# Eleven paired slabs in the second pass of an encoder's down projection, seven of them with weight sums formed by DMA

## The chip, the cores and the metric

The kernel runs on one core of one Trainium2 chip. The metric is the device time in microseconds (us) from launch to end. Engines are named as in the profile: PE (TensorE, matmuls; PEld is its weight load), DVE (VectorE), ACT (ScalarE), POOL (GpSimd), SP (SyncE, which here only issues DMAs).

## The reference

One layer of an encoder with 256 rows (SEQ) of width 2048 in fp32: a mixer of four parallel groups, a cross attention, and a SwiGLU feed-forward network. Only the last matters here, its width D_FF is 5632:

```python
def swiglu(h, w_gate_up, w_down):
    gate, up = jnp.split(h @ w_gate_up, 2, axis=-1)
    return (jax.nn.silu(gate) * up) @ w_down
...
    x = x + swiglu(rms_norm(x, norm_g[l, 2]), w_gate_up[l], w_down[l])
return rms_norm(x, final_norm_g)
```

## The kernel before

**Splits.** All large products are exact to about fp32: each weight w is cast to a shorter format wh on ACT and the rest, wl = w - wh, is formed on DVE. The activations are split in the same way beforehand. A product then takes three matmuls of 128x128 by 512 columns (`part`, L472 hi with wh, L473 hi with wl, L474 lo with wh).

**Slabs.** The weights stream through the core in slabs of 128 x 2048 fp32 (1 MB, 16 blocks of 128 columns), in the order in which PE uses them (`Stream`, from L77). `_load` (L105) issues the DMA of a slab into one of three raw buffers (a fourth, rawx, for most of gate_up). `_plain` (L147) casts and splits half a slab, 1024 columns, at a time (ACT L166, DVE L167). The pairs wh, wl live in a ring of buffers, each one half; the ring has three of its own, and more are lent in parts of the kernel (in down four in all). A buffer comes free when PE has used its half. `_fill` forms the next halves in the program when PE's part of the program needs room; from the last gate_up slabs on, the order of splits on ACT and DVE is fixed to that of the program.

**Pairs.** A plain slab (N in a plan) holds one row block of 2048 columns and takes 8 parts. Two slabs' worth of row blocks k, k+1 and two column groups can also be multiplied as in a Strassen-Winograd scheme, with 7 products instead of 8: a paired slab. It needs sums of the activations (formed by `combine`, L477, on DVE with casts on ACT: two 256-wide additions, four of 128, and splits of 256 and 128) and sums of the weight tiles. `_sums` (L171) yields its halves in four phases of 1024, 512, 1024 and 1024 columns (ACT L178, DVE L179). The sums of weights come in two ways. By DVE: after the second phase four 512-wide additions (L189) form them in place in the raw buffer. By DMA: SP first loads a quarter of the slab, 256 KB, into a tile (L114); ACT copies it (L119); POOL issues an accumulating DMA of 512 KB onto it (L121); the raw load shrinks to 768 KB, and two additions on DVE remain. The tiles for that are the four quarters of the residual, which lies in DRAM during gate_up.

**gate_up** (L1100): eleven groups of 512 gate and 512 up columns. The first is not paired; the other ten have eight slabs each. In before, nine groups follow the plan NSSNSSNN and the last NSNSNSNN, all with sums by DMA. The activations that leave gate_up go through DRAM and come back turned (`fetch`: the tiles f[0] to f[21] in an early generator, f[22] on in another, `rest`, in the last group and in down).

**down** (L1235): two passes of 22 slabs (slabs 208 to 229 and 230 to 251), each over 44 row blocks and two groups of 512 output columns. `paired_rows` (L503) walks over the plan, one letter a slab. In before a plan's S in down means sums by DVE. The first pass has six pairs, NNNNNSNNSNNSNSNNSNNSNN; the second nine, NSNSNSNSNSNSNSNSNSNNNN. A generator `combined` forms the sums of activations (tiles y0 to y7); `before` (in `down`) forces it on when the next slab is a pair whose sum isn't yet made. When a pass's last pair is done, `mixed` (L1257) folds the products into the residual's quarters, and `done` adds the rest and takes squares for the final norm. `down_end` (L1312) does the last products and the norm.

**Order.** Additions, fetches and other work that isn't tied to a slab lies in generators; `Background.poll` puts a step of them into the program after a part, as long as the modelled DVE time owed is under a bound. Each engine runs its own queue in program order. All DMAs of weights go through SP's queue, accumulating loads and the turned activations through POOL's.

Of the kernel before, what the change touches and what calls it, by code (L numbers as in the profile page):

```python
# [19 lines left out]
ALU = mybir.AluOpType  # L20
# [8 lines left out]
FT = DFF // P  # L29
# [10 lines left out]
ROWS = ((0, 512), (704, 1024), (1088, NBLK))  # L40

LATE = 12

GATE_UP = 1920 // 16 + 8
GROUPS = *["NSSNSSNN"] * 9, "NSNSNSNN"

DOWN = GATE_UP + 80
PASSES = "NNNNNSNNSNNSNSNNSNNSNN", "NSNSNSNSNSNSNSNSNSNNNN"

PAIRED = {a + i for a, plan in [(GATE_UP + 8 * j, GROUPS[j % len(GROUPS)]) for j in range(10)] + [(DOWN, PASSES[0]), (DOWN + 22, PASSES[1])]  # L50
          for i, x in enumerate(plan) if x in "Ss"}
AHEAD = (-3, -3)

SUMS = [{GATE_UP + 8 * j + i + a: GATE_UP + 8 * j + i for j in range(10) for i, x in enumerate(GROUPS[j % len(GROUPS)]) if x == "S"}
        for a in AHEAD]

SUMMED = {GATE_UP + 8 * j + i for j in range(10) for i, x in enumerate(GROUPS[j % len(GROUPS)]) if x == "S"}

LAG, OWED, SOON, FAR = 1.3, 0.9, 0.01, 18.0
V_NG = 0  # L60
# [16 lines left out]
class Stream:  # L77
# [27 lines left out]
    def _load(self, n):  # L105

        nc = self.nc
        slot = min(self.raws, key=lambda x: x[1])
        slot[1] = n
        self.raw = slot[0].tile([P, 2048], F32, name="raw", tag="raw")  # L110
        if n // 16 in SUMS[0]:
            t = self.sums[0]
            self.sums.append(self.sums.pop(0))
            nc.sync.dma_start(t[:, 0:512], self.W[SUMS[0][n // 16]][:, 1536:2048])  # L114
            self.begun.append(t)
        if n // 16 in SUMS[1]:
            t = self.begun.pop(0)
            mark = len(nc.cur_bb.bb.instructions)
            nc.scalar.copy(t[:, 512:1024], t[:, 0:512])  # L119
            self.keep(mark)  # L120
            nc.gpsimd.dma_start(t, self.W[SUMS[1][n // 16]][:, 512:1536], accum_op=ALU.add)  # L121
            self.two.append(t)
        if n // 16 in SUMMED:
            nc.sync.dma_start(self.raw[:, 0:1536], self.W[n // 16][:, 0:1536])
            return
        for a, b in zip(CUTS[n], CUTS[n][1:]) if n in CUTS else [(0, 1024), (1024, 2048)] if self.after else [(0, 2048)]:
            (nc.scalar if (n, a) == (0, 0) else nc.sync).dma_start(self.raw[:, a:b], self.W[n // 16][:, a:b])
            if self.after:
                self.after.pop(0)()
# [163 lines left out]
class Block:  # L293
# [563 lines left out]
    def whole(self, c):  # L857
        return self.res[c].rearrange("p k r -> p (k r)")

    def leave(self, c):  # L860
        self.nc.sync.dma_start(self.rd[:, c * 1024:(c + 1) * 1024], self.whole(c))

# [237 lines left out]
    def gate_up(self, gp, f, z):  # L1100

        nc = self.nc
        box, g, stored = {}, {}, []
# [36 lines left out]
        def fetch(k0, k1, ahead, pause, after=0, slow=False):  # L1140

            m = {}
            for k in range(k0, k1 + ahead):
                if k < k1:
                    while len(stored) <= k // 4:
                        yield
                    while after and self.bg.now < stored[k // 4] + after:
                        yield
                    m[k] = self.tmp()
                    mark = self.mark()  # L1150
                    self.load_turned(m[k], self.ff, k)
                    self.keep_place(mark)
                    if slow and k < k0 + ahead - 1:
                        yield
                if k >= k0 + ahead:
                    while k0 == 0 and k - ahead >= 20 and "free" not in box:
                        yield
                    mark = self.mark()
                    self.split(f[k - ahead], m.pop(k - ahead))
                    self.keep_place(mark)  # L1160
                    self.have = k - ahead + 1
                    yield pause
# [21 lines left out]
        sums = [((2 * i, 2 * i + 1), z[(i + 1) % 4]) for i in range(4)]  # L1184
# [19 lines left out]
        self.st.raws.append([rx, -1])  # L1204
        gate(ps[0])
        up(0, ps[1])
        early = fetch(0, FT - 22, 2, 2.0, 12, True)
        self.bg.drain(comb)
        for j in range(1, DFF // 512):
            plan = GROUPS[(j - 1) % len(GROUPS)]  # L1210
            if j == 10:
                box["free"] = True
            turns = [i for i, x in enumerate(plan) if x == "N"][:3]
            if j == 10:
                rest = fetch(FT - 22, FT, 6, SOON, slow=True)

            def begin(i):

                if (j, i) == (10, 5):
                    self.st.back(self.wz, rx)  # L1220
                if i in turns:
                    next(early, None)
                if j == 10 and i > 2:
                    next(rest)

            upped(j, self.paired_rows("w_gate_up", [j * 512, DFF + j * 512], self.h3, sums[:8 - plan.count("N")], plan, mixed, gated,
                                      before=begin, swap=j % 2 == 0)[0])
        more.close()
        for c, x in enumerate(whole):
            nc.sync.dma_start(x, self.rd[:, c * 1024:(c + 1) * 1024])  # L1230
        for _ in early:
            pass
        self.fetch = self.bg.add(rest)
# [1 line left out]
    def down(self, f, sp):  # L1235

        nc, st = self.nc, self.st  # L1240
        ss = self.rp.tile([P, 24], F32, name="rc", tag="rc")
        self.gap(sp, 192)
        z = [sp.tile([P, 768], F32R, name=f"y{i}") for i in range(8)]
        u = sp.tile([P, 512], F32, name="u")
        sums = [((2 * i, 2 * i + 1), z[i % 8]) for i in range(PASSES[1].count("S"))]
        made, split = [], []

        def combined(n):
            for ks, x in sums[len(made):n]:
                yield from self.combine(x, *(f[k] for k in ks))  # L1250
                made.append(x)
                yield 2.0

        def squares(x, c, r):
            nc.scalar.activation(self.tmp().bitcast(BF16), x, AF.Square, accum_out=ss[:, 4 * r + c:4 * r + c + 1])

        def mixed(c, q1, q5, q6, q7):  # L1257

            add = lambda a, b: self.tt(a, a, b, ALU.add)
            nc.scalar.copy(u, q1)  # L1260
            add(self.half(c, 0), u)
            add(u, q6)
            v = [(self.tmp(), slice(j, j + R)) for j in range(0, 512, R)]
            for t, j in v:
                self.tt(t, u[:, j], q7[:, j], ALU.add)
            self.tt(u, q5, u, ALU.subtract)
            add(self.half(c + 1, 0), u)
            for t, j in v:
                add(self.half(c, 1)[:, j], t)
                self.tt(t, q5[:, j], t, ALU.subtract)  # L1270
                add(self.half(c + 1, 1)[:, j], t)
            if c:
                for j in range(0, 512, R):
                    parts = [self.tmp().bitcast(F32R) for _ in range(2)]
                    self.split2(*parts, self.half(3, 1)[:, j:j + R])
                    split.append((j, parts))

        def done(c, *ps):

            for r, p in enumerate(ps):  # L1280
                x = self.half(c, r)
                self.tt(x, x, p, ALU.add)
                squares(x, c, r)

        asked = itertools.count(1)

        def ready(k):

            need = min(FT, max(k + 3, FT - 22 + next(asked) * 3 // 4))
            while self.have < need:  # L1290
                self.bg.step(next(e for e in self.bg.q if e[0] is self.fetch))

        for i, plan in enumerate(PASSES):
            n = plan.count("S")
            g = self.bg.add(combined(n))
            late = (0, LATE)[i]
            plan = plan[:22 - late // 4]

            def before(j):
                while plan[j] == "S" and len(made) <= plan[:j].count("S"):  # L1300
                    self.bg.step(next(e for e in self.bg.q if e[0] is g))
                if late and j == len(plan) - 2:
                    st.back(self.wy)

            ps, rest = self.paired_rows("w_down", [2 * i * 512, (2 * i + 1) * 512], f, sums[:n], plan,
                                        lambda *q: mixed(2 * i, *q), lambda *q: done(2 * i, *q), ready, late, before, i == 1,
                                        () if i else range(2 * n, 2 * n + 8))
            if i == 0:
                done(1, *ps)
        return ss, ps, rest, split  # L1310
# [681 lines left out]
```

## Time and profile before

| | |
|---|---|
| median of three runs | 1428.76 us (1428.35, 1428.76, 1428.78) |
| the profiled execution | 1428.43 us, its span 1426.6 us |
| last gate_up group's end, first pass of down | from about 1185 to 1303 us |
| second pass of down, with the last products | 1303 to 1418 us |
| after PE's last matmul | 8 us |

Times on a timeline count from the start of the span. The busy share of an engine is a mean over the whole span; a window gives the same for a stretch. On a timeline a duration reaches to the end of an instruction, while the next one on the same engine may begin before that; the distance of two starts tells what an instruction takes in a full queue. A wait is named by the engine and line that ended last before the waiting instruction.

### The profile page before, as it was taken

How to read it: one execution, taken by the hardware profiler on the slowest of the kernel's cores; microseconds unless marked ns; L12 is line 12 of the kernel's file. 1: busy time of each engine (PE TensorE's matmuls, PEld its weight loads, DVE VectorE, ACT ScalarE, POOL GpSimd, SP SyncE). 2: the span in 40 equal slices, each digit the busy share in tenths (PEclk: the TensorE clock that was granted, in tenths of full speed). 3: DMA queues.
4: the chain of work that ended last, by engine and by line, in shares of the span. 5: the costliest groups of instructions: out<-in, count | busy, mean ns of one | idle time of the engine just before them, and what ended most of it. 6: DMA issues, size and time to landing. Idle time of an engine off the chain costs nothing.

```text
span 1426.6 us, 18663 instructions
## 1 busy us (share of the span) xinstructions
PE 1416.5 (99%) x6562; PEld 1176.1 (82%) x6562; DVE 1174.3 (82%) x1782; ACT 850.2 (60%) x1242; POOL 243.4 (17%) x315
## 2 busy tenths in 40 slices
PE   9999999999999999999999999999999999999997
PEld 8888888888888888888888888888888888788886
DVE  6667868787878767677578999999999988989997
ACT  7566665445755555555465676667666665655655
POOL 0000100003212233531331121122211024000000
PEclk9999999999999999999999999999999999999999
DMA  9886554457566797965798999999999898665554
GB/s 356 294 291 250 204 198 174 161 177 232 183 216 215 234 278 249 276 197 188 252 298 257 265 280 283 288 291 260 278 291 273 276 276 242 212 235 179 193 220 148
DMA packets 72462, 344.84 MB, mean 242 GB/s; under 512 B 10894, under 2 KB 12591, under 8 KB 45745
## 3 DMA queue, kind: packets, MB, share of 16 engines
q1 hardware_dynamic: 52976, 285.31, 57.4%
q0 software_dynamic: 18960, 57.69, 17.2%
q8 instruction: 51, 0.84, 0.2%
q10 hardware_dynamic: 432, 0.66, 0.1%
q14 instruction: 43, 0.34, 0.1%
HBM read 321.07 MB, written 22.54 MB: 241 GB/s over the span
## 4 chain that ended last, share of the span: by engine, by line
PE 92%; issue 3%; DVE 2%; DMA 2%; POOL 1%; ACT 0%; SPq 0%; DVEq 0%; ACTq 0%; POOLq 0%
PE pg L472 21%; PE pg L474 21%; PE pg L473 21%; PE pm L473 6%; PE pm L474 6%; PE pm L472 6%; PE pg L420 4%; PE pg L421 2%; PE pm L1445 1%; DMA raw<-in_W 1%; PE pm L1074 1%; DMA tmp<-hidden 1%; POOL tmp L605 1%; PE pm L1045 1%; DVE wl L179 0%
## 5 line engine op out<-in xcount | busy, mean ns | idle before, releaser
L167 DVE TENSOR_TENSOR wl<-raw,wh 128x1024 fp32r<-128x1024 f32 (+1 forms) x395 | 473.7, 1212 | 161.3 <-ACT wh L166 159.4
L166 ACT CAST wh<-raw 128x1024 fp32r<-128x1024 f32 (+1 forms) x395 | 406.4, 1042 | 253.0 <-PE pg L474 189.0
L472 PE MATMUL pg<-wh,act 128*128 128x512 f32 (+1 forms) x1165 | 455.5, 391 | 0.0
L474 PE MATMUL pg<-wh,act 128*128 128x512 f32 (+1 forms) x1165 | 453.9, 390 | 0.5 <-DVE act L322 0.5
L473 PE MATMUL pg<-wl,act 128*128 128x512 f32 (+1 forms) x1165 | 453.6, 389 | 0.2 <-DVE wl L167 0.2
L474 PEld LDWEIGHTS pg<-wh,act 128*128 128x128 f32 x1165 | 218.9, 188 | 47.0 <-DVE act L322 1.1
L472 PEld LDWEIGHTS pg<-wh,act 128*128 128x128 f32 x1165 | 219.0, 188 | 46.8 <-issue 1.5
L473 PEld LDWEIGHTS pg<-wl,act 128*128 128x128 f32 x1165 | 219.0, 188 | 45.1 <-DVE wl L167 0.5
L178 ACT CAST wh<-raw 128x1024 fp32r<-128x1024 f32 (+1 forms) x177 | 161.5, 918 | 158.8 <-DVE raw L189 62.7
L179 DVE TENSOR_TENSOR wl<-raw,wh 128x1024 fp32r<-128x1024 f32 (+1 forms) x177 | 182.7, 1057 | 25.7 <-ACT wh L178 24.3
L473 PE MATMUL pm<-wl,act 128*128 128x512 f32 x290 | 112.9, 389 | 0.2 <-DVE wl L167 0.2
L472 PE MATMUL pm<-wh,act 128*128 128x512 f32 x290 | 112.8, 389 | 0.0
L474 PE MATMUL pm<-wh,act 128*128 128x512 f32 x290 | 112.8, 389 | 0.0
L420 PE MATMUL pg<-act,wh 128*128 128x512 f32 x256 | 90.5, 395 | 0.0
L121 POOL DMA_DIRECT2D res<-in_W x39 | 35.0, 897 | 238.3 <-ACT res L119 211.1
L421 PE MATMUL pg<-act,wl 128*128 128x256 f32 x256 | 71.8, 280 | 0.0
L189 DVE TENSOR_TENSOR raw<-raw 128x512 f32<-128x512 f32 x99 | 68.2, 689 | 1.6
L473 PEld LDWEIGHTS pm<-wl,act 128*128 128x128 f32 x290 | 54.4, 188 | 11.8 <-DVE wl L167 0.5
L474 PEld LDWEIGHTS pm<-wh,act 128*128 128x128 f32 x290 | 54.4, 188 | 11.3
L472 PEld LDWEIGHTS pm<-wh,act 128*128 128x128 f32 x290 | 54.4, 188 | 11.3
L420 PEld LDWEIGHTS pg<-act,wh 128*128 128x128 f32 x256 | 48.1, 188 | 10.5
L178 ACT CAST wh<-res 128x1024 fp32r<-128x1024 f32 x39 | 41.2, 1055 | 14.8 <-PE pg L474 4.1
(376 smaller groups left out, 1933.0 us busy)
## 6 DMA issues: line engine op xcount, KB each, us to landing
raw<-in_W SPq DMA_DIRECT2D x207, 1024.0 KB, 5.5
raw<-in_W SPq DMA_DIRECT2D x39, 768.0 KB, 8.9
res<-in_W POOLq DMA_DIRECT2D x39, 512.0 KB, 9.7
res<-in_W SPq DMA_DIRECT2D x39, 256.0 KB, 4.9
raw<-in_W SPq DMA_DIRECT2D x11, 512.0 KB, 7.1
hidden<-g POOLq DMA_DIRECT2D x22, 256.0 KB, 4.0
tmp<-hidden POOLq DMA_DIRECT2D x44, 128.0 KB, 10.5
features<-tmp POOLq DMA_DIRECT2D x32, 128.0 KB, 4.6
```

What stands on the lines that cost most here:

```text
L121: nc.gpsimd.dma_start(t, self.W[SUMS[1][n // 16]][:, 512:1536], accum_op=ALU.add)
L166: nc.scalar.copy(wh[:, a:b], r[:, a:b])
L167: nc.vector.tensor_tensor(out=wl[:, a:b], in0=r[:, a:b], in1=wh[:, a:b].bitcast(F32), op=ALU.subtract)
L178: nc.scalar.copy(wh, src)
L179: nc.vector.tensor_tensor(out=wl, in0=src, in1=wh.bitcast(F32), op=ALU.subtract)
L189: nc.vector.tensor_tensor(out=out, in0=a, in1=b, op=ALU.add)
L420: self.nc.tensor.matmul(p[:, :], wh, slot[:, :], start=start, stop=False)
L421: self.nc.tensor.matmul(p[:, 0:R], wl, slot[:, 0:R], start=False, stop=stop)
L472: self.nc.tensor.matmul(p, hi, wh, start=start, stop=False)
L473: self.nc.tensor.matmul(p, hi, wl, start=False, stop=False)
L474: self.nc.tensor.matmul(p, lo, wh, start=False, stop=stop)
L605: self.nc.gpsimd.dma_start(t.rearrange("p (g t) -> p g t", t=32), src)
```

## The change

- Plans: all ten paired groups of gate_up are NSSNSSNN, so the last has four pairs for three. Down's first pass keeps its six pairs, now written s: sums by DVE. The second pass gets eleven pairs for nine, of which seven (S) have sums by DMA and four (s) by DVE: SSNsSNSsNSNSNSNsNsNNNN.
- Quarters 2 and 3 of the residual stay tiles for weight sums in down. Quarters 0 and 1 are fetched after gate_up, 2 and 3 in the second pass, two slabs after its last S.
- `begins` plans the first step of a tile sum (256 KB load) up to three slabs ahead, not before the tile is free again (four tiles in gate_up, two in down). From the second pass's third S on, the copy and the accumulating load follow one slab after that step.
- Sums of activations: `before` has the generator make all that this slab and the next need; `combined` makes no more than eight ahead of the pairs done, as there are eight tiles for eleven sums.
- The early fetch covers f[0] to f[19] instead of f[21], and the wait on "free" is gone; `ready` counts from 20. The gate_up buffers wz and rawx are given back one slab later in the last group.

```diff
+EARLY = 20
-GROUPS = *["NSSNSSNN"] * 9, "NSNSNSNN"
+GROUPS = "NSSNSSNN",
-PASSES = "NNNNNSNNSNNSNSNNSNNSNN", "NSNSNSNSNSNSNSNSNSNNNN"
+PASSES = "NNNNNsNNsNNsNsNNsNNsNN", "SSNsSNSsNSNSNSNsNsNNNN"
...
+def begins():
+    at = {}
+    for ns, tiles in (([n for n in sorted(SUMMED) if n < DOWN], 4), ([n for n in sorted(SUMMED) if n >= DOWN], 2)):
+        for i, n in enumerate(ns):
+            a = max(n - 3, ns[i - tiles] + 1) if i >= tiles else n - 3
+            assert a not in at and a < n, (a, n)
+            at[a] = n
+    return at
+
+SUMS = begins()
+ADDED = {n: a + (n > DOWN + 23) for a, n in SUMS.items()}
+ADDED = {a: n for n, a in ADDED.items()}
...
-                if (j, i) == (10, 5):
+                if (j, i) == (10, 6):
                     self.st.back(self.wz, rx)
...
-        for c, x in enumerate(whole):
-            nc.sync.dma_start(x, self.rd[:, c * 1024:(c + 1) * 1024])
+        self.fetch_rows((0, 1))
+        self.st.sums = whole[2:]
...
         def combined(n):
             for ks, x in sums[len(made):n]:
+                while len(made) - past[-1] > 7:
+                    yield
...
             def before(j):
-                while plan[j] == "S" and len(made) <= plan[:j].count("S"):
+                past.append(sum(x in "Ss" for x in plan[:j]))
+                while len(made) < sum(x in "Ss" for x in plan[:j + 2]):
                     self.bg.step(next(e for e in self.bg.q if e[0] is g))
+                if i and j == plan.rindex("S") + 2:
+                    self.fetch_rows((2, 3))
```

More of the change, by code (lines that the diff above doesn't have):

```diff
@@ L42 @@
 LATE = 12
+EARLY = 20
 GATE_UP = 1920 // 16 + 8
-GROUPS = *["NSSNSSNN"] * 9, "NSNSNSNN"
+GROUPS = "NSSNSSNN",
 DOWN = GATE_UP + 80
-PASSES = "NNNNNSNNSNNSNSNNSNNSNN", "NSNSNSNSNSNSNSNSNSNNNN"
[L50 to L57, printed above, removed]
+PASSES = "NNNNNsNNsNNsNsNNsNNsNN", "SSNsSNSsNSNSNSNsNsNNNN"
+PLANS = [(GATE_UP + 8 * j, GROUPS[j % len(GROUPS)]) for j in range(10)] + [(DOWN, PASSES[0]), (DOWN + 22, PASSES[1])]
+PAIRED, SUMMED = ({a + i for a, plan in PLANS for i, x in enumerate(plan) if x in kinds} for kinds in ("Ss", "S"))
+def begins():
[9 more added lines that the diff above has]
+ADDED = {a: n for n, a in ADDED.items()}
 LAG, OWED, SOON, FAR = 1.3, 0.9, 0.01, 18.0
@@ L110, in _load @@
         self.raw = slot[0].tile([P, 2048], F32, name="raw", tag="raw")
-        if n // 16 in SUMS[0]:
+        if n // 16 in SUMS:
             t = self.sums[0]
             self.sums.append(self.sums.pop(0))
-            nc.sync.dma_start(t[:, 0:512], self.W[SUMS[0][n // 16]][:, 1536:2048])
+            nc.sync.dma_start(t[:, 0:512], self.W[SUMS[n // 16]][:, 1536:2048])
             self.begun.append(t)
-        if n // 16 in SUMS[1]:
+        if n // 16 in ADDED:
             t = self.begun.pop(0)
@@ L120, in _load @@
             self.keep(mark)
-            nc.gpsimd.dma_start(t, self.W[SUMS[1][n // 16]][:, 512:1536], accum_op=ALU.add)
+            nc.gpsimd.dma_start(t, self.W[ADDED[n // 16]][:, 512:1536], accum_op=ALU.add)
             self.two.append(t)
@@ L858, in whole, with fetch_rows @@
         return self.res[c].rearrange("p k r -> p (k r)")
+    def fetch_rows(self, cs):
+        for c in cs:
+            self.nc.sync.dma_start(self.whole(c), self.rd[:, c * 1024:(c + 1) * 1024])
     def leave(self, c):
@@ L1155, in fetch @@
                 if k >= k0 + ahead:
-                    while k0 == 0 and k - ahead >= 20 and "free" not in box:
-                        yield
                     mark = self.mark()
@@ L1206, in gate_up @@
         up(0, ps[1])
-        early = fetch(0, FT - 22, 2, 2.0, 12, True)
+        early = fetch(0, EARLY, 2, 2.0, 12, True)
         self.bg.drain(comb)
@@ L1210, in gate_up @@
             plan = GROUPS[(j - 1) % len(GROUPS)]
-            if j == 10:
-                box["free"] = True
             turns = [i for i, x in enumerate(plan) if x == "N"][:3]
             if j == 10:
-                rest = fetch(FT - 22, FT, 6, SOON, slow=True)
+                rest = fetch(EARLY, FT, 6, SOON, slow=True)
             def begin(i):
-                if (j, i) == (10, 5):
+                if (j, i) == (10, 6):
                     self.st.back(self.wz, rx)
@@ L1244, in down @@
         u = sp.tile([P, 512], F32, name="u")
-        sums = [((2 * i, 2 * i + 1), z[i % 8]) for i in range(PASSES[1].count("S"))]
-        made, split = [], []
+        sums = [((2 * i, 2 * i + 1), z[i % 8]) for i in range(sum(x in "Ss" for x in PASSES[1]))]
+        made, split, past = [], [], [0]
         def combined(n):
             for ks, x in sums[len(made):n]:
+                while len(made) - past[-1] > 7:
+                    yield
                 yield from self.combine(x, *(f[k] for k in ks))
@@ L1287, in ready @@
         def ready(k):
-            need = min(FT, max(k + 3, FT - 22 + next(asked) * 3 // 4))
+            need = min(FT, max(k + 3, EARLY + next(asked) * 3 // 4))
             while self.have < need:
@@ L1293, in down @@
         for i, plan in enumerate(PASSES):
-            n = plan.count("S")
+            n = sum(x in "Ss" for x in plan)
             g = self.bg.add(combined(n))
@@ L1306, in down @@
                                         lambda *q: mixed(2 * i, *q), lambda *q: done(2 * i, *q), ready, late, before, i == 1,
-                                        () if i else range(2 * n, 2 * n + 8))
+                                        () if i else range(2 * n, EARLY))
             if i == 0:
```

## The prediction

> **What bounds the kernel now.** I first read the busy shares at the head of the page.
>
> ```profile
> span 1426.6 us, 18663 instructions
> PE 1416.5 (99%) x6562; PEld 1176.1 (82%) x6562; DVE 1174.3 (82%) x1782; ACT 850.2 (60%) x1242; POOL 243.4 (17%) x315
> ```
>
> PE is busy for 99% of the span, so in the mean only fewer matmuls could help. The change touches only the last 290 us, and there I read the windows (columns: stretch; sum and PE busy, PEld, DVE, ACT, POOL; PE clock; DMA share; GB/s).
>
> ```profile
> 1161.00:1186.00 25.00, 25.00 (x112) 20.67 (x112) 19.58 (x21) 14.56 (x16) 0.00 (x0) 1.00 0.85 282
> 1226.00:1259.00 33.00, 32.52 (x143) 26.57 (x142) 32.97 (x60) 19.61 (x29) 0.00 (x0) 1.00 0.48 178
> 1270.00:1292.00 22.00, 22.00 (x99) 18.22 (x98) 17.07 (x20) 12.85 (x14) 0.00 (x0) 1.00 0.41 150
> 1292.00:1314.00 22.00, 22.00 (x99) 18.22 (x98) 22.00 (x35) 12.96 (x20) 0.00 (x0) 1.00 0.57 192
> 1314.00:1347.00 33.00, 33.00 (x148) 27.31 (x147) 32.86 (x50) 19.29 (x25) 0.00 (x0) 1.00 0.61 227
> 1358.00:1391.00 33.00, 33.00 (x148) 27.31 (x147) 30.04 (x36) 18.36 (x19) 0.00 (x0) 1.00 0.55 205
> ```
>
> Down's second pass begins at 1303.45. From 1292 to 1347 DVE is as full as PE: 22.00 of 22, then 32.86 of 33. The two engines run neck and neck, with DVE in front by little. So there are two bounds at once: matmuls taken from PE are gained only where the splits (cast by ACT, subtraction by DVE) arrive in step. The waits of PE in the last 250 us show how rarely they fail to now (engine, line waited for: us, times, longest).
>
> ```profile
> PE pg L474 <- DVE act L322: 0.5, 1, 0.5
> PE pm L472 <- ACT y L338: 0.2, 1, 0.2
> PE pm L473 <- DVE wl L167: 0.2, 1, 0.2
> ```
>
> **Prices.** PE's and DVE's busy times overlap from one instruction to the next, so I take distances of starts on the timeline (start, duration, engine, line, operation).
>
> ```profile
> 1303.45 0.39 PE L472 MATMUL pm<-wh,f 128*128 128x512 f32 x1
> 1384.82 0.39 PE L474 MATMUL pg<-wh,y 128*128 128x512 f32 x1
> 1390.26 0.39 PE L474 MATMUL pm<-wh,z 128*128 128x512 f32 x1
> 1299.82 0.41 DVE L322 TENSOR_TENSOR tmp<-pm,tmp 128x256 f32<-128x256 f32 x1
> 1300.16 0.67 DVE L322 TENSOR_TENSOR res<-res,pg 128x512 f32<-128x512 f32 x1
> 1300.75 0.41 DVE L322 TENSOR_TENSOR res<-res,tmp 128x256 f32<-128x256 f32 x1
> 1301.09 2.35 DVE L167 TENSOR_TENSOR wl<-raw,wh 128x1024 fp32r<-128x1024 f32 x2
> 1312.05 2.36 DVE L167 TENSOR_TENSOR wl<-raw,wh 128x1024 fp32r<-128x1024 f32 x2
> 1314.32 1.82 DVE L179 TENSOR_TENSOR wl<-raw,wh 128x1024 fp32r<-128x1024 f32 x2
> 1316.05 0.69 DVE L189 TENSOR_TENSOR raw<-raw 128x512 f32<-128x512 f32 x1
> 1316.66 0.29 DVE L322 TENSOR_TENSOR tmp<-tmp 128x128 f32<-128x128 f32 x1
> 1316.86 0.69 DVE L189 TENSOR_TENSOR raw<-raw 128x512 f32<-128x512 f32 x1
> 1318.26 0.42 DVE L322 TENSOR_TENSOR y<-tmp,y 128x256 fp32r<-128x256 f32 x1
> 1318.60 0.69 DVE L189 TENSOR_TENSOR raw<-raw 128x512 f32<-128x512 f32 x1
> ```
>
> From 1384.82 to 1390.26 lie 24 matmuls: 5.44/24 = 0.227 us each. A plain slab (N, 24 matmuls) is 5.44 us of PE, a paired one (S or s, 21) 4.76. On DVE, two splits of 1024 take 1312.05 to 1314.32, 1.135 each. By starts, a 512-wide operation takes 0.60 (1316.05 to 1316.66), a 128-wide one 0.20, a 256-wide one 0.34. A 512-wide split I take as an add.
>
> The Trainium skill, "VectorE: DVE Perf Modes", section "The TRN2 errata", gives an fp32 tensor_tensor add (N+151)/0.96 ns: 691 for 512 and 1224 for 1024 wide. The durations of the rows agree (0.69, and 2.36 for two), but the next instruction starts 0.09 earlier; a full DVE is priced by starts. Priced by that rule, the 40 operations of the sum below would be 3.6 us longer and the time near 1435 us; the rows decide, so this has no chance of its own.
>
> **The change part by part.**
>
> 1. PE. Three more pairs (one in the last gate_up group, two in the second pass) remove three parts, 9 matmuls: 9 x 0.227 = **-2.04 us**.
>
> 2. The last gate_up group. A fourth pair there adds about 1.7 us of splits and 1.3 of adds to DVE. The window 1161 to 1186 has 5.4 us of DVE idle (19.58 of 25), which hides it: 0. Without that cover it would cost at most these 3 us. The fetches moved (20 early, not 22) and the dropped wait on "free" stand on ACT, DVE and POOL before down begins: also hidden, within the bounds of step 3.
>
> 3. Down's first pass. The sums of activations are now made one slab ahead of need. Before, their lateness made two stalls:
>
> ```profile
> 1214.98 0.48 PE L472 MATMUL pg<-wh,act 128*128 128x512 f32 x1
> 1215.71 0.47 PE L472 MATMUL pm<-wh,y 128*128 128x512 f32 x1 [0.25 <-ACT y L338]
> 1231.46 0.39 PE L474 MATMUL pg<-wh,act 128*128 128x512 f32 x1
> 1232.33 0.50 PE L474 MATMUL pg<-wh,act 128*128 128x512 f32 x1 [0.48 <-DVE act L322]
> ```
>
> The starts lie 0.73 and 0.87 apart instead of about 0.2, so some 0.5 and 0.65 us are lost. The sums' work only moves ahead of splits, on a DVE that is busy for 32.97 of 33 us there, so the splits get late in their place. Behind a late split stand all later splits and, through PE, the release of their buffers. Bounds: both stalls vanish, -1.2, or both stay and one more sum, two 256-wide operations, is in the way, +0.7. I take **+0.2**, near the second, as DVE has no slack.
>
> 4. Second pass, DVE's work at its opening. The old plan began NSNSNSNS, the new one begins SSNsSNSs. A pair with sums by DMA (S) saves two of four adds but has, like every pair, 3.5 half-slabs of splits for 4.76 us of PE: 3 x 1.135 + 0.60 + 2 x 0.60 = 5.2 us of DVE. A plain slab has 2.27 for 5.44. So each S loses 0.45, each s (four adds, 2.78 us by 1316.05 to 1318.60 and its neighbours) about 2, and only N gives 3.2 back. Now the ledger. In before DVE was through with the first pass's last split at 1299.82; nothing ahead of that changes by more than step 3. What must be done before PE can use the third of the four splits of slab 7, the s that stands straight behind an S: 21 splits of 1024 (slabs 0 to 6, and two of slab 7), 6 of 512, 16 adds of sums, 3 closing 512-wide operations of the first pass, 9 of 256 and 12 of 128 wide (closing of the first pass and forming of y sums, which the new plan calls for a slab ahead):
> 21 x 1.135 + (6 + 16 + 3) x 0.60 + 9 x 0.34 + 12 x 0.20 = 23.8 + 15.0 + 3.1 + 2.4 = 44.3 us. DVE, never idle, ends at 1344.1. PE enters at 1303.45 and needs it after five pairs, two plain slabs and ten matmuls: 5 x 4.76 + 2 x 5.44 + 2.27 = 36.95, at 1340.4. **3.7 us late**, and this sum has no idle time in it. Where it comes up: slab 1's tile sums are split, by the same count, 5 x 1.135 + (2 + 4 + 3) x 0.60 + 3 x 0.34 = 12.1 us after 1299.82, at 1311.9, and wanted at matmul 33, 1303.45 + 33 x 0.227 = 1310.9: 1.0 late. With 0.4 in slab 0 (a cast queued behind ACT's squares) and 0.1 in slab 2 the opening costs 1.5; 0.3 in slab 3 and 0.7 in slab 4 follow, and the rest comes up in slab 7.
>
> 5. Slab 7 has a wait of its own. The ring has four halves, so its first half can be cast only when slab 6's first half has been used, six matmuls (1.36) into slab 6 and 3.4 before slab 7. Cast (1.05, row L178 below) and split (1.135) then end 1.2 before slab 7 begins, the 512-wide split 0.6 before; the four adds and one 256-wide operation (2.78 + 0.34) end 2.5 after, the third split 3.7 after. It is wanted at 2.27: 1.4 late, and up to 1.9 when the cast for it queues. Behind it wait slabs 8 on. After that N stands between pairs up to slab 14, DVE recovers (30.04 of 33 in 1358 to 1391), and I count 0.3 to 0.4 for slabs 11 and 12. I take the later end, as ACT holds the y casts too. Together 1.5 + 0.3 + 0.7 + 1.9 + 0.4 = **+4.8**. Bounds: 3.0 if the y sums (2.2 us each: 2 x 0.34 + 4 x 0.20 + 2 x 0.34) fall only into idle time and slab 7 gets its cast early, 6.0 if ACT's casts (row in the rivals) come up to 0.85 late once more.
>
> 6. Second pass, DMA. Seven pairs need a 256 KB load, an ACT copy and a 512 KB accumulating load; their own raw loads shrink to 768 KB.
>
> ```profile
> raw<-in_W SPq DMA_DIRECT2D x207, 1024.0 KB, 5.5
> raw<-in_W SPq DMA_DIRECT2D x39, 768.0 KB, 8.9
> res<-in_W POOLq DMA_DIRECT2D x39, 512.0 KB, 9.7
> res<-in_W SPq DMA_DIRECT2D x39, 256.0 KB, 4.9
> ```
>
> There are two tiles, so a chain can begin when the pair two before it has split its tile: for slab 4 when slab 0's is split, about 1305.8, and it is wanted when slab 4 begins, four slabs on, 1303.45 + 19.7 and the 1.8 that PE is late = 1325. The chain takes 4.9 + 1.1 (copy) + 9.7 = 15.7 of these 19 us. The raw loads: with three buffers a load starts when the slab three before is split, two slabs before its own first cast, 9.5 us where both are pairs. 8.9 leaves 0.6; a quarter load ahead of it in SP's queue (a fourth of 5.5, some 1.3) makes it 0.7 late. In down the DMA engines are busy for 0.57 to 0.61, against 0.85 in gate_up, from which most of these medians come, so I stay near the fast side, the 5.5 of the larger loads: +0.2, bounds 0 and +2.8 (0.7 for each of slabs 1, 4, 6 and 9). The quarters 2 and 3 of the residual come back from the fifteenth slab on; they are wanted in the closing, 30 us later: 0.
>
> 7. The tail: before had a stall of 0.2 at 1394 (third row of the waits) in slabs that are plain in both; -0.2. What follows PE's last matmul is the same.
>
> Sum: -2.04 + 0 + 0.2 + 4.8 + 0.2 - 0.2 = +3.0. On the profiled run, 1428.43 (its span 1426.6 and 1.8 around it), that is 1431.4; the median of before lies 0.33 above that run, so **1431.7 us** for the median. A measurement of this kernel tells about 0.2%, 2.9 us, from no change; the forecast stands at that line.
>
> **Rivals.**
>
> A. The forecast: DVE is late at the opening and in slab 7. Net +1.2 to +4.2, 1430 to 1433. Chance 0.66, about half of it over 0.2%.
>
> B. The DMA bound. If the 768 KB loads land as in gate_up, each of four pairs is 0.7 late by step 6, and the casts behind it, on one ACT queue, wait too: 2.8 instead of 0.2, 1434.3. The point is a landing of about 8.2 us. For it: the median of 8.9. Against: the DMA share of the windows. ACT's casts would show it:
>
> ```profile
> L178 ACT CAST wh<-raw 128x1024 fp32r<-128x1024 f32 x27 | 28.3, 1050 | 27.4 <-DVE raw L189 19.6 <-PE pm L474 6.0 <-PE pg L474 1.7
> ```
>
> Now (1290 to 1395) they wait for adds of DVE (19.6) and the ring, and for no load. The Trainium skill, "DMA: Bandwidth & Descriptors", section "Anatomy of one DMA — SWDGE (gpsimd) path", fits such a transfer with 2.0 us and the bytes over 436 GB/s, an estimate of 3.2 us for 512 KB; the row's 9.7 disagrees. By that rule the chain would be done in 9 us and only the raw loads could bring B. Chance 0.15.
>
> C. The other side: DVE keeps up. The price is DVE's place at the start of the pass. In 1270 to 1292 it idles for 4.9 us (17.07 of 22). If the new order lets DVE use it, by forming y sums there, and it enters the pass 3.7 us earlier, the ledger closes; from there on only the matmuls count: 1428.76 - 2.04 - 0.2, less up to 1.2 of step 3: 1425.3 to 1426.6. Against it: idle there is the ring being full, and the sums that a plan of one slab ahead asks for are few. Chance 0.09.
>
> D. Between: half of the lateness is absorbed, +0.4 to +1.2 net, within 0.2%. Chance 0.10.
>
> **How the numbers follow.** Faster by over 0.2% is C's better part, 0.06; slower by over 0.2% is B and half of A, 0.15 + 0.34 = 0.49; the rest, 0.45, is within 0.2%. The range leaves out C and the far end of B: 1428.9 (D's lower part) to 1434.8 (B with A's far end cut).
>
> **What would show it.** Right: PE waits for wl and wh between 1305 and 1347 of some 4.5 us, the largest in slab 1 (near 1311) and slab 7 (near 1341), DVE full from 1292 to 1347; 9 matmuls fewer; no stall over 0.5 before 1200. Wrong: ACT casts that wait for a load or for the accumulated tile (B); DVE idle in the opening (C); stalls in the first pass beyond 2 us; a longer wait for residual quarters at the end.

## The result, and the profile after

| | before | after |
|---|---|---|
| median | 1428.76 us (5 runs, 1428.35 to 1428.83) | 1435.05 us (5 runs, 1433.16 to 1435.21) |
| profiled execution | 1428.43, span 1426.6 | 1435.21, span 1433.2 |
| PE's last matmul starts | 1418.40 | 1424.67 |

The change makes the kernel slower: ratio 1.004 with a 95% interval of 1.0029 to 1.0051, 6.3 us by the medians. That is the forecast's direction, at twice its size (+3.0), and 0.25 us above the range's top. Lines of code have moved: L472 to L474 are now L483 to L485, L166 and L167 are L177 and L178, L178, L179 and L189 are L189, L190 and L200, L119 is L130, L322 is L333 and L338 is L349.

The waits of PE from 1180 us on in the changed kernel (line waited for: us, times, longest):

```profile
PE pg L483 <- ACT wh L189: 1.9, 3, 1.1
PE pm L484 <- DVE wl L190: 1.8, 1, 1.8
PE pm L483 <- ACT wh L189: 0.9, 1, 0.9
PE pg L484 <- DVE wl L190: 0.5, 1, 0.5
PE pm L484 <- DVE wl L178: 0.3, 1, 0.3
PE pm L1362 <- ACT tmp L349: 0.2, 1, 0.2
```

Before had three such rows with 0.9 us in all. Five of the six speak of casts and splits of weights that came late. The second one, a single wait of 1.8, lies in the first pass, where the forecast had none of that size. The windows show both places, and something else:

```profile
1226.00:1259.00 33.00, 31.24 (x131) 25.12 (x130) 32.46 (x61) 19.32 (x32) 0.00 (x0) 0.95 0.47 178
1292.00:1314.00 22.00, 20.95 (x92) 16.67 (x90) 21.76 (x33) 13.22 (x21) 0.54 (x1) 1.00 0.67 202
1314.00:1347.00 33.00, 31.14 (x133) 24.66 (x134) 32.86 (x53) 21.52 (x31) 2.52 (x3) 1.00 0.84 238
```

DVE stays full in 1314 to 1347 (32.86 of 33, as before), while PE falls from 33.00 to 31.14. In 1226 to 1259 the granted clock is 0.95, where it was 1.00.

To place every loss I sum up, over a stretch, by how much the distance of two matmul starts exceeds 0.23 us (in proportion less after a matmul of fewer than 512 columns); for short this is called the stall sum. Its differences and the matmuls saved should give the whole difference:

| stretch of the profiled execution | before | after | forecast of the difference |
|---|---|---|---|
| down's first pass, 1200 to 1303 | 1.35 | 3.77 | +0.2 |
| second pass, 1303 to 1400 | 0.20 | 5.37 | +4.8 + 0.2 - 0.2 |
| end, from 1400 | 0.86 | 1.36 | 0 |
| 9 matmuls | | -2.04 | -2.04 |

The differences, 2.42 + 5.17 + 0.50 - 2.04 = 6.05, are the 6.27 by which PE's last matmul is later, but for 0.2 that the sums don't place.

**The second pass** went as the ledger had it, slab by slab. The timeline of PE (with the idle time just before and what ended it), slab 1 first, then slab 7:

```profile
1314.16 0.50 PE L483 MATMUL pg<-wh,y 128*128 128x512 f32 x1 [1.07 <-ACT wh L189]
...
1345.18 0.50 PE L483 MATMUL pg<-wh,y 128*128 128x512 f32 x1 [0.41 <-ACT wh L189]
...
1346.79 0.50 PE L483 MATMUL pm<-wh,f 128*128 128x512 f32 x1 [0.87 <-ACT wh L189]
```

And DVE's timeline in slab 7, from its 1024- and 512-wide splits through the four additions to the third split:

```profile
1340.61 1.83 DVE L190 TENSOR_TENSOR wl<-raw,wh 128x1024 fp32r<-128x1024 f32 x2
1342.35 0.68 DVE L200 TENSOR_TENSOR raw<-raw 128x512 f32<-128x512 f32 x1
1342.95 0.42 DVE L333 TENSOR_TENSOR y<-tmp,y 128x256 fp32r<-128x256 f32 x1
1343.29 0.69 DVE L200 TENSOR_TENSOR raw<-raw 128x512 f32<-128x512 f32 x1
1343.89 0.28 DVE L333 TENSOR_TENSOR y<-tmp,y 128x128 fp32r<-128x128 f32 x1
1344.09 0.68 DVE L200 TENSOR_TENSOR raw<-raw 128x512 f32<-128x512 f32 x1
1344.69 0.28 DVE L333 TENSOR_TENSOR f<-tmp,f 128x128 fp32r<-128x128 f32 x1
1344.90 0.68 DVE L200 TENSOR_TENSOR raw<-raw 128x512 f32<-128x512 f32 x1
1345.50 1.22 DVE L190 TENSOR_TENSOR wl<-raw,wh 128x1024 fp32r<-128x1024 f32 x1
```

There is no gap in this queue: additions and pieces of a y sum alternate, and the third cast can start only behind the additions it reads. Stalls by start distance: 0.30 in slab 0 (forecast 0.4), 1.23 in slab 1 (1.0), 0.57 in slab 4 (0.7), 0.57 + 1.04 in slab 7 (1.4 to 1.9), 0.64 + 0.18 in slabs 11 and 12 (0.3 to 0.4), and some 0.1 each behind a stall. The 0.3 that was forecast for slab 3 did not come.

**The first pass.** PE stops once for 2.03 us, and then runs at half speed: from 1235.01 on, matmuls start 0.43 apart instead of 0.23 (PE's timeline).

```profile
1230.68 0.49 PE L483 MATMUL pm<-wh,y 128*128 128x512 f32 x1
1232.94 0.50 PE L484 MATMUL pm<-wl,y 128*128 128x512 f32 x1 [1.76 <-DVE wl L190]
...
1235.43 0.63 PE L483 MATMUL pm<-wh,y 128*128 128x512 f32 x1
1235.86 0.63 PE L484 MATMUL pm<-wl,y 128*128 128x512 f32 x1
1236.29 0.63 PE L485 MATMUL pm<-wh,y 128*128 128x512 f32 x1
```

Some 1.5 us of the stretch's 3.77 are that half speed. The stall is in slab 8, a pair. ACT's timeline shows what its first cast waited for, first in before, then in after:

```profile
1222.93 1.05 ACT L178 CAST wh<-raw 128x1024 fp32r<-128x1024 f32 x1 [1.09 <-DMA raw<-in_W]
```

```profile
1223.95 1.05 ACT L189 CAST wh<-raw 128x1024 fp32r<-128x1024 f32 x1 [3.77 <-DMA raw<-in_W]
```

The cast waits for a raw load, and DVE, which is full behind it (32.46 of 33 in the window above), does not make up for it before PE's stall. In the chains of waits of the same stretch it stands as one piece, before and after:

```profile
1216.42 6.41 DMA raw<-in_W
```

```profile
1215.91 7.95 DMA raw<-in_W
```

The buffer came free 0.5 us earlier than before, and the load landed 1.0 later. Its slab's buffer is that of slab 5, also a pair, which holds it to its last split.

### The profile page after: what moved, and what is told of

It reads as the page before. It is cut to its first block, busy times and chain, and to the rows that moved or that the text cites. A ratio compares the mean times of both kernels' runs of the same rounds, so it can differ in the third digit from the quotient of the medians.

```text
span 1433.2 us, 18748 instructions
## 1 busy us (share of the span) xinstructions
PE 1417.9 (99%) x6553; PEld 1174.7 (82%) x6553; DVE 1181.7 (82%) x1802; ACT 858.9 (60%) x1262; POOL 250.2 (17%) x323
## 4 chain that ended last, share of the span: by engine, by line
PE 86%; DVE 6%; issue 4%; DMA 2%; ACT 1%; POOL 1%; SPq 0%; ACTq 0%; DVEq 0%; POOLq 0%
PE pg L484 20%; PE pg L483 20%; PE pg L485 20%; PE pm L484 5%; PE pm L485 5%; PE pm L483 5%; PE pg L431 4%; PE pg L432 2%; DVE wl L190 2%; DMA raw<-in_W 1%; DVE raw L200 1%; PE pm L1462 1%; DVE wl L178 1%; PE pm L1090 1%; DMA tmp<-hidden 1%
## 5 line engine op out<-in xcount | busy, mean ns | idle before, releaser
L178 DVE TENSOR_TENSOR wl<-raw,wh 128x1024 fp32r<-128x1024 f32 (+1 forms) x389 | 466.7, 1212 | 155.5 <-ACT wh L177 153.4
L177 ACT CAST wh<-raw 128x1024 fp32r<-128x1024 f32 (+1 forms) x389 | 400.0, 1042 | 241.5 <-PE pg L485 183.1
L483 PE MATMUL pg<-wh,act 128*128 128x512 f32 (+1 forms) x1166 | 455.9, 391 | 0.1
L485 PE MATMUL pg<-wh,act 128*128 128x512 f32 (+1 forms) x1166 | 454.3, 390 | 0.0
L189 ACT CAST wh<-raw 128x1024 fp32r<-128x1024 f32 (+1 forms) x181 | 163.5, 913 | 161.6 <-DVE raw L200 63.3
L483 PEld LDWEIGHTS pg<-wh,act 128*128 128x128 f32 x1166 | 219.2, 188 | 46.9 <-issue 1.5
L485 PEld LDWEIGHTS pg<-wh,act 128*128 128x128 f32 x1166 | 219.2, 188 | 46.0 <-DVE act L333 0.2
L190 DVE TENSOR_TENSOR wl<-raw,wh 128x1024 fp32r<-128x1024 f32 (+1 forms) x181 | 185.5, 1052 | 31.6 <-ACT wh L189 30.2
L483 PE MATMUL pm<-wh,act 128*128 128x512 f32 x284 | 110.6, 390 | 0.1
L485 PE MATMUL pm<-wh,act 128*128 128x512 f32 x284 | 110.5, 389 | 0.0
L132 POOL DMA_DIRECT2D res<-in_W x47 | 41.5, 882 | 377.6 <-ACT res L130 343.2
L189 ACT CAST wh<-res 128x1024 fp32r<-128x1024 f32 x47 | 49.6, 1055 | 22.2 <-PE pm L485 6.9
L483 PEld LDWEIGHTS pm<-wh,act 128*128 128x128 f32 x284 | 53.3, 188 | 11.6 <-ACT wh L189 0.6
L485 PEld LDWEIGHTS pm<-wh,act 128*128 128x128 f32 x284 | 53.3, 188 | 11.0
L200 DVE TENSOR_TENSOR raw<-raw 128x512 f32<-128x512 f32 x87 | 59.8, 688 | 1.6
L190 DVE TENSOR_TENSOR wl<-res,wh 128x1024 fp32r<-128x1024 f32 x47 | 57.1, 1215 | 0.0
```

What stands on the lines that cost most here:

```text
L132: nc.gpsimd.dma_start(t, self.W[ADDED[n // 16]][:, 512:1536], accum_op=ALU.add)
L177: nc.scalar.copy(wh[:, a:b], r[:, a:b])
L178: nc.vector.tensor_tensor(out=wl[:, a:b], in0=r[:, a:b], in1=wh[:, a:b].bitcast(F32), op=ALU.subtract)
L189: nc.scalar.copy(wh, src)
L190: nc.vector.tensor_tensor(out=wl, in0=src, in1=wh.bitcast(F32), op=ALU.subtract)
L200: nc.vector.tensor_tensor(out=out, in0=a, in1=b, op=ALU.add)
```

## The experiments

Profiles of the experiments are read by the same stall sums. The first 300 us of all these kernels are the same work, and their stall sum there differs by up to 1.3 us between the profiles: that much of a single time is no effect of an edit.

**1. Sums of activations by need in the first pass.**

```diff
-                while len(made) < sum(x in "Ss" for x in plan[:j + 2]):
+                while len(made) < sum(x in "Ss" for x in plan[:j + 1 + i]):
```

> The change, but in down's first pass the sums of activations are again made only when the next slab needs them; the second pass still makes them a slab ahead. Theory (DVE's place sets the first pass; one stall of 2.0 us there is followed by about 3 us of matmuls at half speed): the one stall is split again into two of 0.5 and about 1.2, nothing runs at half speed, and the time falls by about 1.5 from 1435.05 to some 1433.5. Rival (the order of the sums itself costs 2 us of stall): 1432.5 or less. Rival (the first pass does not matter for the end, the second pass's DVE would be late anyway): 1435, unchanged.

Median 1434.6 (1433.05 to 1435.49), ratio to before 1.004 (1.0026 to 1.0053): by the time alone not told from the change. The profile tells more: 0.53 and 1.36 instead of one stall of 2.03, nothing at half speed, a stall sum of 2.22 for 3.77, and 5.30 in the second pass. Its first 300 us were 1.0 longer than the change's, which hides most of the 1.55. The order of the sums places the stall; it doesn't make it.

**2 to 4. The second pass: its order or its DMAs.** The plans of the second pass:

```diff
-"SSNsSNSsNSNSNSNsNsNNNN"
+"NsNsNsNsNsNsNsNsNsNNNN"   (run 2: nine pairs, all by DVE, as before)
+"NSNSNSNSNSNSNSNsNsNNNN"   (run 3: nine pairs, seven by DMA)
+"ssNssNssNsNsNsNsNsNNNN"   (run 4: the change's order, all by DVE)
```

Runs 2 and 4 have no S, so there the residual's quarters 2 and 3 are fetched at slab 15 by its number, the slab of the change.

> The change with the second pass's plan of before (nine pairs alternating with plain slabs, all sums by DVE, no tile sums by DMA in down). Theory (5.3 us of stalls come from the second pass's order): they go and 6 matmuls (1.4 us) come back, so 1435.05 - 5.3 + 1.4 = about 1431.1; PE waits in the second pass under 0.5 in all. Rival (the loss comes from the first pass and gate_up, and the second pass only shows it): 1434 or more.

> The second pass of before in its order (nine pairs alternating with plain slabs), but seven of them with sums by DMA. Theory (it is the order of the slabs, not the DMA): stalls in the second pass of 0 to 1.6 us, time within 1.6 of the old second pass's, about 1431 to 1432.7. Rival (tile sums and 768 KB loads by DMA arrive late, or hold up ACT): stalls of 3 us or more, 1434 and up.

> The eleven pairs in the change's order, but all sums by DVE, no tile sums by DMA in down. Theory (DVE is the bound at the opening; DMA saves it two adds of 0.6 per pair, some of which only fills idle time): 3 to 6 us slower than the change, 1438 to 1441. Rival (the tile sums by DMA are what costs): faster than the change, 1431 to 1434.

| | median | ratio to before | stall sum, first pass | second pass |
|---|---|---|---|---|
| 2 | 1430.19 | 1.0008 (1.0000 to 1.0017) | 4.38, half speed | 0.00 |
| 3 | 1430.86 | 1.0013 (1.0004 to 1.0021) | 2.47 | 0.00 |
| 4 | 1439.3 | 1.0072 (1.0059 to 1.0085) | 2.57 | 9.01 |

The plan it is, not its DMAs. Alternating with plain slabs, nine pairs run without a stall whether their sums come by DVE or by DMA; in the change's order the loss is 5.37 with DMA sums and 9.01 without. Runs 2 and 3 take away two pairs together with the order; run 6 below changes the order alone. The first long stall of run 4 in PE's timeline is the ledger's cast behind four additions, now in slab 0:

```profile
1309.09 0.50 PE L483 MATMUL pm<-wh,act 128*128 128x512 f32 x1 [1.40 <-ACT wh L189]
```

Seven DMA sums are worth 3.6 us in this order and nothing in the other, where DVE has the time. In all three the first pass has the stall of 2.03.

**5. First pairs later.**

```diff
-PASSES = "NNNNNsNNsNNsNsNNsNNsNN", ...
+PASSES = "NNNNNNNsNNsNsNNsNsNsNN", ...
```

> The change with the first pass's six pairs moved back: the first pair at slab 7 instead of 5, no pair before slab 7, the last at slab 19 as before (NNNNNNNsNNsNsNNsNsNsNN). Theory (the first pass's stall of 2.0 us is DVE's place after gate_up, and two more plain slabs let it catch up): nearly no stall in the first pass, 2.2 to 3.8 us less than the change, 1431.3 to 1432.9; the second pass keeps its 5.3. Rival (the second pass's stalls are inherited from the first): they shrink too, time under 1430. Rival (DVE is late at both ends in any order): 1435.

Median 1430.93 (1429.98 to 1432.51), ratio 1.0015 (1.0006 to 1.0024). The first pass's stall sum is 0.00, the second's 5.34, unchanged. So the second pass inherits nothing, and the two losses add: by the medians run 5 is 4.1 us faster than the change, which is about the whole loss of the first pass, the stall, the half speed and the 1.35 that before had there too.

**6. Slabs 7 and 8 exchanged.**

```diff
-"SSNsSNSsNSNSNSNsNsNNNN"
+"SSNsSNSNsSNSNSNsNsNNNN"
```

> The change with slabs 7 and 8 of the second pass exchanged (SSNsSNSNsSNS... instead of SSNsSNSsNSNS...), so that a plain slab stands between the pair with sums by DMA and the one with four adds. Theory (slab 7 pays for its own ring wait, 1.4 to 1.9): the two stalls there, 0.57 + 1.04, go for the most part; 1.2 to 1.8 us less than the change, 1433.3 to 1433.9. Rival (the lateness is the sum of DVE work and only moves to the next pair): stalls move to slabs 8 to 11 and the time stays at 1435.

Median 1433.21 (1432.38 to 1434.25), ratio 1.003 (1.0019 to 1.0042). The stalls at slabs 7 and 11 are gone, the sum is 3.28 instead of 5.37, and those of slabs 0, 1 and 4 stay as they were. In its waits of PE, the casts (ACT L189) are now named twice for 1.5 us, where the change had four such waits for 2.8; the first pass's 1.8 is still there:

```profile
PE pm L484 <- DVE wl L190: 1.8, 1, 1.8
PE pg L483 <- ACT wh L189: 1.5, 2, 1.1
```

With the same DVE work in the pass, 2.1 us less: slab 7's loss was its place behind an S, as the forecast's step 5 had it, and was not handed on.

**7. Three pairs in the last gate_up group.**

```diff
-GROUPS = "NSSNSSNN",
+GROUPS = *["NSSNSSNN"] * 9, "NSNSNSNN"
```

> The change with three pairs in the last gate_up group, as before, so 3 matmuls (0.68 us) more. Theory (the first pass is bound by DVE, which takes back what PE gains in front of it): the stall of 2.0 us in the first pass shrinks by as much, and the time is that of the change within 0.3, or up to 1.5 lower where no half-speed stretch follows. Rival (the fourth pair is a real gain): 0.7 slower, 1435.7.

Median 1435.43 (1434.21 to 1437.58), ratio 1.0046 (1.0034 to 1.0059). The stall did not shrink: 2.03 again, with another of 0.68 just ahead of it. My theory, that DVE takes back what PE gains, fell with that. Together with ACT's wait for the raw load it gave a new one: in this stretch the DMA engines are full, in before almost as much as in after, and the change has put more on them. The windows 1204 to 1216 and 1216 to 1224, first before, then after (columns as in the forecast's windows; the last but one is the DMA share):

```profile
1204.00:1216.00 12.00, 11.75 (x52) 9.37 (x51) 11.18 (x20) 6.71 (x13) 4.41 (x5) 1.00 1.02 264
1216.00:1224.00 8.00, 8.00 (x37) 6.59 (x36) 7.31 (x13) 5.56 (x9) 0.00 (x0) 1.00 0.95 260
```

```profile
1204.00:1216.00 12.00, 12.00 (x55) 9.93 (x54) 11.86 (x25) 7.51 (x14) 6.17 (x7) 1.00 1.02 260
1216.00:1224.00 8.00, 8.00 (x37) 6.64 (x36) 6.42 (x11) 3.25 (x6) 0.00 (x0) 1.00 1.02 273
```

The DMA issues of 1208 to 1226, before and after (count, KB each, median us to landing, which for the raw loads the trace has for one of three and two of three):

```profile
raw<-in_W SPq DMA_DIRECT2D x3, 1024.0 KB, 6.3
tmp<-hidden POOLq DMA_DIRECT2D x3, 128.0 KB, 10.6
```

```profile
raw<-in_W SPq DMA_DIRECT2D x3, 1024.0 KB, 8.1
tmp<-hidden POOLq DMA_DIRECT2D x5, 128.0 KB, 10.6
```

Five turned loads of activations instead of three, and raw loads of 8.1 instead of 6.3; run 7 has six, and 8.3. They are more because the change fetches 20 tiles early where before fetched 22, so two more come here.

**8 to 10. The two early tiles back, and a better plan.** Run 9 is run 7 with EARLY at 22 and the wait on "free" restored:

```diff
-EARLY = 20
+EARLY = 22
...
+                    while k0 == 0 and k - ahead >= 20 and "free" not in box:
+                        yield
...
+            if j == 10:
+                box["free"] = True
```

> The change with three pairs in the last gate_up group and, as before, 22 turned activation tiles fetched early (with the wait on free), so that 22 and not 24 are left for the end of gate_up and down; the rest of the change stays. Theory (the raw load of the ninth slab of down's first pass, a pair, lands late, 8 us after its buffer is free, because more turned loads stand on DMA engines that are full there; before it took 6.4): the load takes 6.4 to 7 and PE's stall of 2.03 us falls to 1.2 or less. Rival (DVE's own work, four adds and sums a slab ahead, makes the stall): 2.0 as in the run with three pairs. Time 0.7 to 1.5 below the run with three pairs, or the same.

Median 1433.54 (1433.37 to 1433.93), ratio 1.0029 (1.0017 to 1.0041). ACT's first cast of slab 8 in run 7, then in run 9, and after them the chain of waits and the DMA issues of run 9:

```profile
1225.40 1.05 ACT L189 CAST wh<-raw 128x1024 fp32r<-128x1024 f32 x1 [5.01 <-DMA raw<-in_W]
```

```profile
1223.05 1.05 ACT L189 CAST wh<-raw 128x1024 fp32r<-128x1024 f32 x1 [2.72 <-DMA raw<-in_W]
```

```profile
1216.80 6.16 DMA raw<-in_W
```

```profile
raw<-in_W SPq DMA_DIRECT2D x3, 1024.0 KB, 6.7
tmp<-hidden POOLq DMA_DIRECT2D x4, 128.0 KB, 10.4
```

The cast of slab 8 starts 2.35 us earlier than in run 7, the load took 6.16 us, and PE's stall is 0.63 instead of 0.68 + 2.03; the sum of the first pass is 1.27, and 1.35 in before. Run 7 has the same gate_up plan, the same sums a slab ahead and the same four additions; by the medians run 9 is 1.9 us faster. The two tiles moved out of the early fetch made the first pass's loss. (The wait on "free" holds only these two tiles. EARLY at 22 also moves the row blocks 20 and 21 to the front of the first pass's plain slabs, which was not tried apart.)

Run 8 takes run 5's first pass, and in the second pass nine pairs that begin with a pair (SNSNSNSNSNSNsNsNsNNNNN). Run 10 has SNSNsNSNsNSNsNsNsNNNNN.

> First pass as in the run with its pairs later, second pass with nine pairs that alternate with plain slabs and begin with a pair: SNSNSNSNSNSNsNsNsNNNNN, six with sums by DMA; the last pair is one slab earlier than before's. Against before only 3 matmuls fewer (0.68 us). Theory (PE bound as soon as DVE has its plain slabs): no stall in the first pass (1.3 less than before), none or up to 1.5 in the second, and 0.5 to 1.0 less at the end, as the closing work of DVE is over earlier: 1425.7 to 1427.2. Rival (sums by DMA late at this spacing): 1428 and more.

> The run with nine spread pairs, with three DMA-summed pairs (third, fifth and so on) turned to sums by DVE: second pass SNSNsNSNsNSNsNsNsNNNNN, four pairs with sums by DMA. Theory (its one stall, 0.93 us in slab 4, is the third tile sum, whose tile comes free too late): no stall over 0.3 us after 1100, 0.9 below that run, 1426.2 to 1427 by the median and 1425.7 to 1426 by a profiled run. Rival (DVE is late there, more with four adds): a stall of 1 us or more stays at slab 4, no gain.

(Run 10 turned two pairs, the third and fifth of the six with sums by DMA, not three.) Run 8: median 1427.76 (1426.61 to 1429.66), ratio 0.9992 (0.9983 to 1.0001), not told from before; one stall, 0.93 in slab 4, the rest 0.3. Run 10: median 1425.93 (1425.51 to 1427.28), ratio 0.9978 (0.9970 to 0.9987): faster than both kernels, with a stall sum of 0.18 from 1100 us to the end. The window of 1186 to 1303 shows a PE without a gap:

```profile
1186.00:1303.00 117.00, 117.00 (x518) 96.89 (x517) 108.44 (x181) 69.38 (x106) 20.00 (x23) 1.00 0.72 227
```

The stall of run 8 went with the two sums, but not quite for the reason that I gave. The tile that comes free late is that of a later sum, and what it holds up is ACT: the copy of that sum waits for its quarter load, and the casts of slab 4 stand behind it in the queue:

```profile
1317.11 0.62 ACT L130 COPY res<-res 128x512 f32<-128x512 f32 x1 [1.71 <-DMA res<-in_W]
1317.64 1.56 ACT L189 CAST wh<-raw 128x1024 fp32r<-128x1024 f32 x2
```

So a load can hold up casts on ACT's one queue, as rival B has it, though here a quarter load does it and not a raw one. The change itself has this too, in slab 11 (under step 6 below).

## Why the prediction was right, and where it was not

- **Step 1, 9 matmuls, -2.04:** right; PE's instructions fell from 6562 to 6553.
- **Steps 4 and 5, the opening and slab 7, +4.8:** right in mechanism and place, and near in size: the stalls up to slab 7 add up to 4.3 us, and the two steps have 4.4 for them. The whole pass lost 5.17 more than before; slabs 11 and 12 cost 0.4 more than forecast, for a reason that stands under step 6. Runs 3 and 4 tell the plan from the DMAs, and run 6 tells slab 7's own wait from the rest. One count beside the sum is wrong: it has 67 operations, not 40, so that 0.09 more for each would be 6.0 us and a time near 1437.7. That the 1435 named there is close to the measured time is chance.
- **Step 6, DMA in the second pass, +0.2:** too low, and its reason does not hold. The DMA share of that stretch rose from 0.61 to 0.84, which the forecast had not worked out, and the 768 KB loads came close to the rival's point of 8.2 (DMA issues of after, 1295 to 1400):

```profile
raw<-in_W SPq DMA_DIRECT2D x6, 768.0 KB, 8.1
res<-in_W POOLq DMA_DIRECT2D x5, 512.0 KB, 7.9
```

  Two waits of ACT for a load show. A cast at 1298.55, ahead of the pass, waits 2.88 us for its raw load, and DVE is full behind it (21.76 of 22 in 1292 to 1314). The other one costs PE time. A quarter load starts when its tile is free, as the step had it, but the copy that waits for it stands on ACT's queue ahead of the casts of slab 11, which are wanted sooner. The chain of waits, ACT's timeline and PE's stall in slab 11, all in after:

```profile
1354.76 5.16 DMA res<-in_W
```

```profile
1360.00 0.62 ACT L130 COPY res<-res 128x512 f32<-128x512 f32 x1 [1.66 <-DMA res<-in_W]
```

```profile
1369.11 0.50 PE L484 MATMUL pg<-wl,y 128*128 128x512 f32 x1 [0.48 <-DVE wl L190]
```

  The five profiles with this second pass bear it out: where the copy waits 1.66, 1.55, 1.52, 1.36 and 1.05 us (after, runs 5, 9, 1 and 7), slab 11 stalls for 0.64, 0.53, 0.50, 0.35 and 0.1. Run 4, with the same order and no such load, has no stall there. So about 0.6 of the pass's 5.17 belongs to this step; the 0.9 of run 8 is the same.
- **Step 2, "The fetches moved (20 early, not 22) ... also hidden":** this is the step that failed, and with it step 3's +0.2. I looked at DVE's slack and at the order of the sums; the cost went through the DMA engines, which are full there (1.02), and a raw load that takes 1.5 us longer in a slab that has no slack. The stretch cost 2.42 more than before, not 0.2; about 0.9 of it is stall and 1.5 the half speed that followed. Run 9 shows the cause, runs 1 and 7 rule out the order of sums and the fourth pair as its source. The forecast's own sign of being wrong, stalls in the first pass beyond 2 us, turned up with 2.03.
- **Step 7:** the 0.2 at 1394 went, as forecast, but the row of waits that the step quotes is another: it lies at 1403.00 in before, and stayed (0.29 at 1407.53 in after). The end from 1400 on lost 0.50 more than before, which no step had; runs 5, 7 and 9, with the same second pass, lose less than 0.1 more there. In run 10, whose last pair is one slab earlier, the stall sum there is 0.01; what made the 0.50 in this one profile wasn't taken apart.
- **Rival C** asked for a DVE that gains 3.7 us ahead of the pass. In the change DVE idles for 5.2 us of 1270 to 1292 (16.79 busy of 22), as it did before, so the idle time was not used. Run 5 gives the pass an entry with no stall ahead and it loses 5.34 all the same. A DVE that enters 3.7 us ahead was not tried.

The half-speed stretch comes in some executions and not in others. It follows the stall of 2.03 in the profiles of after and of runs 2 and 6, and doesn't in runs 3, 4 and 7 with the same stall. No kernel without that stall shows it (before, runs 1, 5, 8, 9, 10). The clock records of the traces answer most of this. Every stretch of constant clock between a kernel's first and last change of it is a whole multiple of 3.413 us long (1228.80 is 360 of them, 191.15 is 56), so the clock is set in steps of that length, and where they begin differs from execution to execution. The stall's step and the next one, in after and then in run 3 (the last but two is the PE clock):

```profile
1230.90:1234.31 3.41, 1.65 (x7) 1.05 (x6) 3.41 (x7) 3.18 (x5) 0.00 (x0) 1.00 0.00 0
1234.31:1237.72 3.41, 3.41 (x10) 2.63 (x9) 3.41 (x5) 2.07 (x3) 0.00 (x0) 0.50 0.66 211
```

```profile
1229.67:1233.08 3.41, 1.81 (x7) 0.94 (x5) 3.41 (x8) 3.15 (x5) 0.00 (x0) 1.00 0.00 0
1233.08:1236.49 3.41, 3.25 (x14) 2.51 (x15) 3.41 (x6) 2.96 (x5) 0.00 (x0) 1.00 0.28 46
```

In after and in runs 2 and 6 PE's whole wait falls into one step, PE is busy for 1.57 to 1.65 us of it, and the next step has half the clock. In runs 3, 4 and 7 a border of the steps cuts the wait, PE is busy for 1.81 us or more, and the clock stays. No other step of the twelve profiles, from 15 us on to PE's last matmul, has a PE busy for less than 1.81. So the same wait costs some 1.5 us more or nothing, by where it falls. This fits all twelve profiles, but no run moved the wait against the steps by itself.

## What to carry to other kernels

Where two engines run neck and neck, saved work on one is worth what the other can deliver slab by slab: count the feeding engine's work up to each deadline, as the ledger did, and put the cheap slabs between the dear ones before adding dear ones. Ask of every transfer that is moved later which stretch it lands in, and whether the DMA engines are full there, even if its own data is not urgent. Nine pairs in a good order lose next to nothing in the second pass (runs 3 and 10), eleven in the change's order lose 5 us; eleven in a good order were not tried, but one exchange of two slabs gave back 2.1 (run 6).

## What the runs showed of the hardware

- After a stall of 2.03 us (PE idle for 1.76), PE's matmuls of 512 columns started 0.427 apart for some 3 us, beginning 2 us behind the stall's end; the granted clock is 0.50 over one step of 3.41 us there. It came in three of six profiles with such a stall, those in which the whole wait lies in one step, and in no place after a stall of 1.57 us or less. The Trainium skill, "TensorE: Matmul & The Clock Gate", section "HAM oscillation — how this bites in real kernels", warns of gaps of over 3.4 us; the measurement has the same effect after 2.03, and decides.
- Beside two more turned loads of 128 KB each, among full DMA engines, a 1 MB load took 7.95 us instead of 6.41, more than their bytes would suggest (256 KB at the 273 GB/s of that window are about 1 us); with the two taken back (run 9) it took 6.16.
- A copy on ACT that waits 1.05 to 1.66 us for a load holds up the casts behind it in the queue: PE then stalls for 0.1 to 0.64 us (slab 11, above).
